# Second norm of both borders by columns: eight columns of sums, root and reciprocal, spread by a product with diagonals, and a new order list

## The chip, the cores and the metric

The kernel runs on one core of one Trainium2 chip. The metric is the time of an execution on the device in microseconds (us). TensorE is called PE here, VectorE DVE, ScalarE ACT, GpSimd POOL, and SyncE, which only issues DMAs, SP.

## The reference

One encoder layer on 512 tokens of width 1024, of three sublayers. Each has the same frame:

```
h = rms_norm(x, g) * (1 + scale) + shift
y = rms_norm(fn(h), g2)
x = x + w * gate * y
```

`fn` is a SwiGLU feed-forward in the first and third sublayer (hidden width 2816) and a mixer in the second: one projection gives queries, keys, values and two recurrent branches; four heads of differential attention and a gated recurrence in both directions run beside each other, and an output projection joins them. `scale`, `shift` and `gate` come from a conditioning vector. The norm divides each token by the root of its mean square over the 1024 channels plus 1e-6.

## The kernel before

**Layout.** Channels lie on the 128 partitions, tokens along the free dimension: the residual is a tile `X` of eight blocks (k = 0 to 7) of 128x512. A sum over channels is therefore a sum over partitions, made by PE with a matrix of ones. Each f32 product is made of three in fp32r (`mm3`, L177 to L179): high part of the weights by high part of the data, low by high, high by low. ACT makes the high part of a weight tile (L206, steps `ws`), DVE or POOL the low part (L214, steps `wl`), from a tile that a DMA staged (steps `wd`). There are three tiles of each kind, so `ws` of a unit waits until PE is done with the unit three before.

**The borders.** A border is the passage from one sublayer to the next; border 1 stands ahead of the mixer, border 2 ahead of the second feed-forward. Its steps, in the names of the code (a step is `name.border.half.block`, and `half` is left out where all 512 tokens are meant):

- `pt`: the last output tile of the sublayer, in two halves of 256 tokens. `qs` squares it on ACT; `sa` (L869) and `sn` (L872) sum the squares over the partitions on PE, `sa` those of the tiles before and `sn` that of the last one; `sq` takes the root on ACT. That is the first norm, of the sublayer's output.
- `xm`, `xf`, `xg`: `X` is scaled and the output added, on DVE or POOL. `uh` and `ul` make the high and low part of `X` for the next projection, which starts before the second norm is known: `kq` and `kk.k` multiply block k of the seven first weight tiles, and `gm.0` to `gm.6` add the last block tile by tile. The seven sums fill seven of the eight PSUM banks; `sh` (L419) makes seven columns for the shift, `sw` copies them.
- `sx`, `sax`: squares of `X` on ACT, added up on DVE or POOL. `e2` (L931, L932) makes the epsilon's share, 128x512. `ss` (L945, L946): two products with the matrix of ones put the sum of squares of each token into all 128 partitions of a bank, 128x512. `sd` (L970, DVE) scales and adds the epsilon's share, `sr` (L975, ACT) takes the root, `rv` (L978, DVE) the reciprocal, all on 128x512. That is the second norm, `r12`.
- `hm.k` (L982): `X` block k times `r12`, from SBUF; `hf`, `hh`, `hl` scale and shift it and split it into high and low part. Those are the data of the further projections (`pj`, `vp`, `tt`). The seven sums are scaled by `r12` when they are taken out of PSUM: `xs` and `rs` in border 1 (L1019), `sg` in border 2 (L1472).

**Behind border 1.** `xs.i` scales a tile of the recurrent branch, `xa.i` (ACT) adds the shift, `cd.i` is its convolution on DVE (L1274 and three L1278), `ch.i` (ACT, L1301) and `cl.i` (DVE, L811) its high and low part. `ga.ik` are the gate products of tile i, each of two times three products, with `gs` (ACT, a sigmoid) behind them. `ga.00` is the first thing that PE does after `gm.6`. The attention (`sc` scores, `mx` maxima, `ex` exponentials, `w1` and `w2` weights, `tp` transposes, `pv` values, `ms` to `mu` a norm by columns) and the recurrence (`le` to `ls`) follow, then the output projection `mo`, `mp`.

The attention's norm is already made by columns: `ms` (L1219) sums into eight columns, `me` (L1223, ACT) takes the root of 128x8, `rc` (L1227, DVE) the reciprocal, `dx` (L1233, ACT) makes four diagonals and `rb` (L1237) spreads them by one product with ones.

**The order.** Everything from the last part of the first feed-forward's output to the first tiles of the second feed-forward is issued in an order written out by hand or by a search, the list `MIXER` of some 880 steps. The program issues the steps one after another, and each engine works its own instructions off in that sequence. A suffix `.p` puts a step on POOL, `.d` on DVE. An instruction that waits holds up all that stand behind it on its engine.

Of the kernel before, what the change touches and what calls it, by code (L numbers as in the profile page):

```python
# [76 lines left out]
xm.1.1.3 gh.1 xg.1.7 xg.1.3 uh.1.2.3 xm.1.1.5 xg.1.5 wd.-1 wd.0 sax.1.1 sax.1.2 kq.1.2 kq.1.3 ws.-1 sx.1.4
sx.1.3 sx.1.5 gh.0 uh.1.2.7 ul.1.2.3 sax.1.3 wl.-1 xg.1.6 kq.1.4 sax.1.4 sax.1.5.p ul.1.2.4 kk.1.2 kk.1.3 wd.1
sx.1.6 sax.1.6 sx.1.7 sw.1 sfree.1 e2.1.p ws.0 uh.1.2.6 uh.1.2.5 wl.0 wd.2 ul.1.2.5 ws.1 ss.1 ws.2 sd.1
ul.1.2.7 sr.1 rv.1 wd.3 hm.1.1 xq kk.1.4 hf.1.1 ul.1.2.6 hm.1.3 hm.1.4 hf.1.3 hm.1.2 hh.1.1 hm.1.7 hm.1.6  # L80
gl.0.p hm.1.0 hf.1.7 wl.1.p wl.2.p ws.3 kk.1.5 wd.4 wd.5 hm.1.5 kk.1.6 hf.1.2.d wl.3 wd.6 gm.1.0 gm.1.1 gm.1.2
# [1570 lines left out]
```

## Time and profile before

| | us |
|---|---|
| median of 3 runs | 985.12 |
| lowest, highest | 984.38, 986.12 |
| the profiled execution, its own time | 985.61 |
| its span in the trace | 983.8 |
| busy in that span: PE, DVE, ACT, POOL | 957.7, 595.8, 432.3, 201.2 |

Border 1 lies at about 365 to 426 us of the span, the gates, the attention and the recurrence from there to about 573, border 2 at about 594 to 644. A row of a view gives the line of the code, the engine, the operation with what it writes and reads, the shape and how often it came; rows of the timeline give the start and the duration in us; a bracket at the end gives the idle time of the engine before the row and what ended it. Matmuls overlap, so that a row is longer than the distance to the next one; on the chain of waits each stands with the time that it adds.

### The profile page before, as it was taken

How to read it: one execution, taken by the hardware profiler on the slowest of the kernel's cores; microseconds unless marked ns; L12 is line 12 of the kernel's file. 1: busy time of each engine (PE TensorE's matmuls, PEld its weight loads, DVE VectorE, ACT ScalarE, POOL GpSimd, SP SyncE). 2: the span in 40 equal slices, each digit the busy share in tenths (PEclk: the TensorE clock that was granted, in tenths of full speed). 3: DMA queues.
4: the chain of work that ended last, by engine and by line, in shares of the span. 5: the costliest groups of instructions: out<-in, count | busy, mean ns of one | idle time of the engine just before them, and what ended most of it. 6: DMA issues, size and time to landing. Idle time of an engine off the chain costs nothing.

```text
span 983.8 us, 11742 instructions
## 1 busy us (share of the span) xinstructions
PE 957.7 (97%) x4480; PEld 789.3 (80%) x4480; DVE 595.8 (61%) x814; ACT 432.3 (44%) x668; POOL 201.2 (20%) x138
## 2 busy tenths in 40 slices
PE   7999999999999999989999999999999999999994
PEld 4888888888888889867777779788888888888883
DVE  7977656566666656998899647984333333322216
ACT  5662332335222234589988766552223322222230
POOL 1007300000000123434667332252200000001014
PEclk9999999999999999989999999999999999999998
DMA  8836555555688872223221231332232323333312
GB/s 308 313 132 231 208 185 199 201 193 176 222 277 268 291 214 67 90 64 107 78 84 32 65 121 57 102 108 90 103 107 85 108 89 99 86 95 98 97 38 86
DMA packets 45002, 137.10 MB, mean 139 GB/s; under 512 B 7185, under 2 KB 9745, under 8 KB 44946
## 3 DMA queue, kind: packets, MB, share of 16 engines
q1 hardware_dynamic: 44082, 135.62, 41.3%
q8 instruction: 35, 0.57, 0.2%
q10 hardware_dynamic: 864, 0.74, 0.2%
q14 instruction: 21, 0.17, 0.1%
HBM read 132.14 MB, written 2.10 MB: 136 GB/s over the span
## 4 chain that ended last, share of the span: by engine, by line
PE 94%; DVE 4%; DMA 1%; SPq 0%; issue 0%; ACT 0%; DVEq 0%; ACTq 0%
PE PS L177 30%; PE PS L179 30%; PE PS L178 30%; PE PS L1146 1%; PE PS L1183 1%; DVE s L1574 1%; DVE s L1577 1%; DMA X<-in_xT 1%; DVE s L1278 0%; PE PS L1219 0%; DVE s L1569 0%; PE PS L1237 0%; PE PS L476 0%; PE PS L419 0%; PE PS L872 0%; SPq L465 0%
## 5 line engine op out<-in xcount | busy, mean ns | idle before, releaser
L177 PE MATMUL PS<-s,wh 128*128 128x512 f32 (+1 forms) x1032 | 394.3, 382 | 0.1
L179 PE MATMUL PS<-s,wh 128*128 128x512 f32 (+1 forms) x1032 | 391.9, 380 | 0.0
L178 PE MATMUL PS<-s,wl 128*128 128x512 f32 (+1 forms) x1032 | 391.7, 380 | 0.0
L214 DVE TENSOR_TENSOR wl<-st,wh 128x1024 fp32r<-128x1024 f32 (+3 forms) x148 | 178.4, 1207 | 191.0 <-ACT wh L206 190.8
L206 ACT ACTIVATE wh<-st 128x1024 fp32r<-128x1024 f32 (+2 forms) x170 | 170.3, 1002 | 127.7 <-PE PS L179 115.1
L177 PEld LDWEIGHTS PS<-s,wh 128*128 128x128 f32 x1032 | 194.1, 188 | 38.7 <-issue 1.0
L179 PEld LDWEIGHTS PS<-s,wh 128*128 128x128 f32 x1032 | 194.0, 188 | 37.2 <-DVE s L542 0.4
L178 PEld LDWEIGHTS PS<-s,wl 128*128 128x128 f32 x1032 | 194.1, 188 | 36.9 <-issue 0.5
L177 PE MATMUL PS<-q,wh 128*128 128x512 f32 (+1 forms) x288 | 107.0, 371 | 0.0
L179 PE MATMUL PS<-q,wh 128*128 128x512 f32 (+1 forms) x288 | 106.0, 368 | 0.0
L178 PE MATMUL PS<-q,wl 128*128 128x512 f32 (+1 forms) x288 | 105.9, 368 | 0.0
L729 POOL TENSOR_TENSOR s<-s,s 128x512 f32<-128x512 f32 x12 | 16.1, 1341 | 385.6 <-ACT s L725 385.6
L259 DVE CUSTOM_DVE_ANT_0 q<-q,q 128x1024 bf16<-128x1024 f32 x72 | 89.7, 1246 | 0.2 <-DMA q<-in_w_ada 0.2
L649 ACT ACTIVATE s<-PS 128x512 f32<-128x512 f32 x39 | 23.3, 596 | 101.8 <-PE PS L179 101.7
L654 DVE TENSOR_TENSOR s<-s,PS 128x512 f32<-128x512 f32 x40 | 27.4, 685 | 65.9 <-PE PS L179 65.2
L214 POOL TENSOR_TENSOR wl<-st,wh 128x1024 fp32r<-128x1024 f32 (+3 forms) x21 | 50.7, 2422 | 61.0 <-ACT wh L206 61.0
L177 PEld LDWEIGHTS PS<-q,wh 128*128 128x128 f32 x288 | 54.2, 188 | 9.8 <-ACT s L1385 0.4
L179 PEld LDWEIGHTS PS<-q,wh 128*128 128x128 f32 x288 | 54.1, 188 | 9.8 <-POOL q L811 0.3
L178 PEld LDWEIGHTS PS<-q,wl 128*128 128x128 f32 x288 | 54.2, 188 | 9.6
L625 ACT ACTIVATE q<-s 128x512 fp32r<-128x512 f32 x24 | 15.2, 632 | 95.4 <-DVE s L654 95.4
L625 ACT ACTIVATE s<-s 128x512 fp32r<-128x512 f32 x16 | 10.1, 632 | 70.4 <-DVE s L654 70.4
L414 DVE SCALAR_TENSOR_TENSOR s<-st,ada,s 128x512 f32<-128x512 f32 (+1 forms) x28 | 19.7, 743 | 26.6 <-DMA st<-in_wma 13.4
(241 smaller groups left out, 922.0 us busy)
## 6 DMA issues: line engine op xcount, KB each, us to landing
q<-in_w_ada SPq DMA_DIRECT2D x72, 512.0 KB, 3.8
st<-in_w2b SPq DMA_DIRECT2D x37, 512.0 KB, 3.3
st<-in_w1b SPq DMA_DIRECT2D x36, 512.0 KB, 4.5
st<-in_w1o SPq DMA_DIRECT2D x16, 512.0 KB, 4.5
st<-in_w2o SPq DMA_DIRECT2D x16, 512.0 KB, 3.5
st<-in_wma SPq DMA_DIRECT2D x16, 448.0 KB, 4.1
st<-in_w2a SPq DMA_DIRECT2D x16, 448.0 KB, 3.4
st<-in_wmb SPq DMA_DIRECT2D x9, 512.0 KB, 3.4
```

Of the source, the lines that this page charges most:

```text
L177: PE.matmul(o, wh, ah, start=start, stop=False)
L178: PE.matmul(o, wl, ah, start=False, stop=False)
L179: PE.matmul(o, wh, al, start=False, stop=stop)
L206: ACT.activation(h[:, :n], staged[i][:, :n], AF.Copy)
L214: eng.tensor_tensor(out=l[:, :n], in0=st[:, :n], in1=h[:, :n].bitcast(F32), op=ALU.subtract)
L259: DVE.tensor_tensor_reduce(out=junk, in0=t, in1=cond, op0=ALU.mult, op1=ALU.add, scale=1.0, scalar=0.0, accum_out=ada[:, i:i + 1])
L414: DVE.scalar_tensor_tensor(out=o, in0=i, scalar=colS(j, k), in1=o, op0=ALU.mult, op1=ALU.add)
L625: ACT.activation(h, t, AF.Copy)
L649: ACT.activation(t, PS[:, b], AF.Silu)
L654: DVE.tensor_tensor(out=g, in0=g, in1=PS[:, b], op=ALU.mult)
L729: POOL.tensor_tensor(out=st["acc"], in0=st["acc"], in1=t, op=ALU.add)
L1146: PE.matmul(PS[:, b[m]], qs[x][part, c], ks[y][part], start=i == 0, stop=i == 2)
```

## The change

The second norm of both borders goes the way of the attention's norm. `e2` keeps only its first step, on one partition (1x512). `ss` becomes twelve products of two columns: for each of the four groups of 128 tokens one with the epsilon's row (one partition, against a new constant `epsd`) and two with the sums of squares, all into eight columns of one bank. `sd` is now the root of 128x8 on ACT, `sr` a reciprocal of 128x8 and four diagonals of 128x128 on DVE, `rv` one product of 128x512 on PE, which spreads the diagonals over all partitions of the same bank. `hm` reads this bank instead of a tile in SBUF and always runs on DVE; a new step `rw` copies the bank to SBUF on ACT, for `xs`, `rs` and `sg`, and a new step `ub` gives the bank back, later than before. Nothing else is computed otherwise.

```
-ws.-5 lt.1 dq pt.1.0.0 sa.1.0 wl.-5.p pt.1.0.1 pt.1.0.2 pt.1.1.0 qs.1.0 sn.1.0 pt.1.1.1 pt.1.1.2 wd.-4 wd.-3
+pt.1.0.0 ws.-5 lt.1 pt.1.0.1 wl.-5.p pt.1.0.2 wd.-4 sa.1.1 qs.1.0 sa.1.0 sn.1.0 sq.1.0 xm.1.0.0.p xm.1.0.5
...
+    epsd = one.tile([128, 2], F32, name="epsd")
...
+    DVE.memset(epsd, EPS * D)
...
         def e2(e, b):
             t, s1 = ar.s(), B["s1", b]
             G[b].E2 = t
-            e.tensor_tensor(out=t, in0=s1, in1=s1, op=ALU.mult)
-            e.tensor_scalar(out=t, in0=t, scalar1=EPS, scalar2=0.0, op0=ALU.mult, op1=ALU.add)
+            e.tensor_tensor(out=t[0:1], in0=s1[0:1], in1=s1[0:1], op=ALU.mult)
...
         def ss(e, b):
             k = G[b].sb = bank()
-            t, q = B["sx", b, 0], B["sx", b, 7]
-            PE.matmul(PS[:, k], ones, t, start=True, stop=False)
-            PE.matmul(PS[:, k], ones, q, start=False, stop=True)
-            ar.give(t, q)
+            t, q, E2 = B["sx", b, 0], B["sx", b, 7], G[b].E2
+            for a, c in ((E2[0:1], epsd[0:1]), (t, ones[:, 0:2]), (q, ones[:, 0:2])):
+                for i in range(4):
+                    PE.matmul(PS[:, k, 2 * i:2 * i + 2], a[:, 128 * i:128 * i + 128], c, start=a is not t and a is not q and i == 0,
+                              stop=a is q and i == 3)
+            ar.give(t, q, E2)
...
         def sd(e, b):
             g = G[b]
+            g.rt = smp.tile([128, 8], F32, tag="rt", name="rt", bufs=1)
+            ACT.activation(g.rt, PS[:, g.sb, 0:8], AF.Sqrt, scale=1.0 / D)
+
+        def sr(e, b):
+            g = G[b]
             g.r12 = ar.s()
-            DVE.scalar_tensor_tensor(out=g.r12, in0=PS[:, g.sb], scalar=1.0 / D, in1=g.E2, op0=ALU.mult, op1=ALU.add)
-            unbank(g.sb)
-            ar.give(g.E2)
-
-        def sr(e, b):
-            ACT.activation(G[b].r12, G[b].r12, AF.Sqrt)
+            DVE.reciprocal(g.rt, g.rt)
+            for i in range(4):
+                DVE.tensor_scalar(out=g.r12[:, 128 * i:128 * i + 128], in0=ident, scalar1=g.rt[:, 2 * i:2 * i + 1], scalar2=None,
+                                  op0=ALU.mult)
 
         def rv(e, b):
-            DVE.reciprocal(G[b].r12, G[b].r12)
+
+            PE.matmul(PS[:, G[b].sb], ones, G[b].r12, start=True, stop=True)
+
+        def rw(e, b):
+            ACT.activation(G[b].r12, PS[:, G[b].sb], AF.Copy)
+
+        def ub(e, b):
+            unbank(G[b].sb)
 
         def hm(e, b, k):
             ht[b, k] = ar.s()
-            e.tensor_tensor(out=ht[b, k], in0=X[:, k], in1=G[b].r12, op=ALU.mult)
+            DVE.tensor_tensor(out=ht[b, k], in0=X[:, k], in1=PS[:, G[b].sb], op=ALU.mult)
```

The whole list `MIXER` is another one, with 882 steps. Line numbers behind the new code are higher: by 2 or 3 in the first part, so that `mm3` is L179 to L181, `sa` L872, `sn` L875 and `sh` L422, and by 15 behind the border. In the new kernel `ss` is L950, `sd` L975, `sr` L980 and L982, `rv` L987, `rw` L990 and `hm` L997. Three places of the new order are shown. The number behind the name of a tile tells one use of a slot from another.

**PE at the second border, around `ss.2`.** First before: the last product of a block of `kk`, the two products of the sum, and the next block.

```order
L179 MATMUL PS<-s_4879,wh 128x512
L945 MATMUL PS<-s_4845,ones 128x512
L946 MATMUL PS<-s_4956,ones 128x512
L177 MATMUL PS<-s_4912,wh 128x512
L178 MATMUL PS<-s_4912,wl 128x512
L179 MATMUL PS<-s_4913,wh 128x512
```

Now the same place; `s_5046` are the four diagonals.

```order
L181 MATMUL PS<-s_4972,wh 128x512
L950 MATMUL PS<-epsd,s_5017 128x2 x4
L950 MATMUL PS<-ones,s_4963 128x2 x4
L950 MATMUL PS<-ones,s_5007 128x2 x4
L987 MATMUL PS<-s_5046,ones 128x512
L179 MATMUL PS<-s_5014,wh 128x512
L180 MATMUL PS<-s_5014,wl 128x512
L181 MATMUL PS<-s_5015,wh 128x512
```

Here `rv.2` (L987) follows `ss.2` at once, and `kk.2.4` stands behind it. `ss.2` stands behind `kk.2.3`, one block later than before. In border 1 the block `kk.1.4` stands between `ss.1` and `rv.1`.

**DVE at the first border, from the first `xs` to the low part for the gate.** Before: three scalings of tiles from PSUM, two convolutions, and the low part `cl.0` (L811).

```order
L1019 TENSOR_TENSOR s_3185<-PS,s_3057 128x512
L1019 TENSOR_TENSOR s_3188<-PS,s_3057 128x512
L1019 TENSOR_TENSOR s_3192<-PS,s_3057 128x512
L1274 TENSOR_SCALAR s_3206<-q_3066,par 128x512
L1278 SCALAR_TENSOR_TENSOR s_3206<-q_3066,par,s_3206 128x510
L1278 SCALAR_TENSOR_TENSOR s_3206<-q_3066,par,s_3206 128x511 x2
L1274 TENSOR_SCALAR s_3220<-q_3066,par 128x512
L1278 SCALAR_TENSOR_TENSOR s_3220<-q_3066,par,s_3220 128x510
L1278 SCALAR_TENSOR_TENSOR s_3220<-q_3066,par,s_3220 128x511 x2
L811 TENSOR_TENSOR s_3212<-s_3206,s_3211 128x512
```

Now (L1034 are the scalings, L216 is `wl.5`, L814 is `cl.0`):

```order
L1034 TENSOR_TENSOR s_3230<-PS,s_3095 128x512
L216 TENSOR_TENSOR wl<-st,wh 128x1024
L1034 TENSOR_TENSOR s_3242<-PS,s_3095 128x512
L1289 TENSOR_SCALAR s_3246<-q_2820,par 128x512
L1293 SCALAR_TENSOR_TENSOR s_3246<-q_2820,par,s_3246 128x510
L1293 SCALAR_TENSOR_TENSOR s_3246<-q_2820,par,s_3246 128x511 x2
L1034 TENSOR_TENSOR s_3252<-PS,s_3095 128x512
L814 TENSOR_TENSOR s_3255<-s_3246,s_3254 128x512
```

The second convolution now stands behind the low part, and the low part `wl.5` of a weight tile stands among the scalings.

**PE at the end of the sublayer's last tile, border 1, second half.** Before: the last product of the tile, `sa.1.1`, `sn.1.1`, then the columns of the shift (`sh.1`).

```order
L179 MATMUL PS<-s_1886,wh 128x256
L869 MATMUL PS<-s_1992,ones 128x256
L872 MATMUL PS<-s_2644,ones 128x256
L419 MATMUL PS<-ones,s_1963 128x2 x4
L419 MATMUL PS<-ones,s_1964 128x2 x3
```

Now:

```order
L181 MATMUL PS<-s_1888,wh 128x256
L422 MATMUL PS<-ones,s_1965 128x2 x4
L422 MATMUL PS<-ones,s_1966 128x2 x3
L875 MATMUL PS<-s_2670,ones 128x256
L179 MATMUL PS<-s_2802,wh 128x256
```

The columns of the shift moved ahead of `sn`; `sa.1.1` was made with the first half. At border 2 `sh.2` stands ahead of `sa.2.1` and `sn.2.1` too, and `pt.2.1.0` ahead of `sa.2.0` and `sn.2.0`.

More of the change, by code (lines that the diff above doesn't have):

```diff
@@ L77 @@
[L77 to L81, printed above, removed]
@@ L122 @@
[L122 to L123 removed]
+pt.1.0.0 ws.-5 lt.1 pt.1.0.1 wl.-5.p pt.1.0.2 wd.-4 sa.1.1 qs.1.0 sa.1.0 sn.1.0 sq.1.0 xm.1.0.0.p xm.1.0.5
+xm.1.0.7.p pt.1.1.0 ws.-4 pt.1.1.1 xm.1.0.1.p pt.1.1.2 lfree.1 wd.-3 wd.-2 xf.1.0.0 uh.1.0.0 xm.1.0.4
+xf.1.0.1.p uh.1.0.1 ul.1.0.0 sh.1 xm.1.0.2 xm.1.0.6 xq ul.1.0.1 ws.-3 qs.1.1 xm.1.0.3.p wl.-4 wl.-3 sn.1.1
@@ new lines @@
+ul.1.2.6 kk.1.4 gh.0 gl.0 sd.1 sr.1 ul.1.2.7 rv.1 wl.1 wd.4 wl.2 hm.1.4 kk.1.5 ws.3 hf.1.4 wl.3.p hm.1.7
+hm.1.3 hf.1.3 hm.1.0 hh.1.3 hm.1.2 hm.1.5 wd.5 hf.1.0.d kk.1.6 hh.1.4 hm.1.1 gl.1.p rawfree gm.1.0 gm.1.1
+gm.1.2 hl.1.3.p hf.1.5.d hf.1.2 gm.1.3 gm.1.4 wd.6 gm.1.5 hh.1.2 hl.1.2 hf.1.7 hl.1.4 dq gm.1.6 hh.1.7 hh.1.5
+ws.4 hm.1.6 hf.1.6 wl.4 rw.1 ws.5 xs.0 wl.5 xa.0 ub.1 hl.1.5.p hh.1.6 hh.1.0 xs.2 xa.2 hl.1.7.p cd.0 hf.1.1
+rs.k0 ch.0 cl.0 hh.1.1 hl.1.1.p xs.3 xs.1 ra.k0 rd.k0 ga.00 ws.6 rs.q1 xa.1 gs.00 rs.q0 cd.2 xa.3 ch.2 ga.01
@@ new lines @@
+wr.12 pv.2 po.2 ge.3 lh.1 ll.1 ah.0 ex.13 ll.2.p mo.0 w2.14 lf.3 w1.12 w2.12 mo.2 wr.13 mo.1 ws.20 lh.3
+wl.20.p w1.13 w2.13 wd.22 ms.2 tp.12 ex.15 tp.14 me.2 tp.13 th.13 ll.3 wr.15 ws.21 th.14 al.0 w1.15.p mo.3
+w2.15 tp.15 wd.23 ws.22 wl.21 tl.13 rc.2 ah.1 th.15 tl.14 mo.4 zF.k3 tl.15 dx.2 th.12 ws.23 wl.22.p hfree
+tl.12 wd.24 rb.2 ws.24 al.1 mu.2 ah.2 wl.23.p pv.3 lt.2 po.3 mo.5 wd.25 ws.25 wd.26 ms.3 me.3 al.2 wl.24.p
+rc.3 mo.6 dx.3 rb.3 wl.25.p mu.3 ws.26 ah.3 wd.27 al.3 mp.4 mo.7 wl.26 ws.27 mp.5 pf.0 pf.1 zF.q3 wd.28 ws.28
@@ new lines @@
+wd.29 wl.27 wl.28 vfree ws.29 mp.6 pf.2 pf.3 pt.2.0.0 pf.4 pf.5 pa.1.p pt.2.0.1 pa.2.p pt.2.0.2 wd.30 ws.30
+wd.31 pa.3.p wl.29.p pf.6 rr pa.4 pt.2.0.3 pa.5 pa.6 pt.2.1.0 sa.2.0 qs.2.0 sn.2.0 sq.2.0 wl.30 so.0 pt.2.1.1
+xm.2.0.0 qkfree.3 xf.2.0.0 uh.2.0.0 pt.2.1.2 xm.2.0.4 xm.2.0.3 pt.2.1.3 qs.2.1 xm.2.0.2 wd.32 ul.2.0.0
+xm.2.0.1 sh.2 xm.2.0.5 wd.33 sa.2.1 xf.2.0.1 sn.2.1 sq.2.1 uh.2.0.1 so.1 ws.31 xm.2.1.2 ul.2.0.1 xm.2.1.0
+xf.2.1.0.p xm.2.1.1 uh.2.1.0 xg.2.2 ul.2.1.0 xf.2.1.1.p uh.2.1.1 ul.2.1.1 xm.2.1.3 xm.2.0.6 xm.2.1.6 lfree.2
@@ L124 @@
+ws.37 hm.2.1 hm.2.6 wl.36.p hm.2.2 wd.38 hf.2.1.d hm.2.5 kk.2.6 rw.2 wd.39 gm.2.0 hf.2.2.d hh.2.2 hh.2.3
+hf.2.6 hh.2.6 gm.2.1 hl.2.3.p hl.2.4.p ws.38 wl.37 wd.40 hh.2.1 hl.2.6 gm.2.2 gm.2.3 hf.2.7 gm.2.4 hl.2.0.p
+gm.2.5 gm.2.6 sg.0 sl.0 gfree.2 hf.2.5 hh.2.5 hh.2.7 ws.39 sg.2 hl.2.1.p sg.4 hl.2.2.p sl.4 sg.5 tt.7.0 sg.3
+sg.6 sl.6 sl.2 wl.38 hl.2.5.p sg.1 ofree ub.2 pg.0 hl.2.7.p tt.7.1 ws.40 pg.1 pg.2 tt.8.0 wl.39 p3 ph.0 wd.41
+ph.3 ph.1 tt.8.1 pl.1 ph.2 wl.40 pl.2 pl.3 p4 pl.0 r2free
 """.split()
```

76 lines of the change are left out of this document (30 added, 46 removed).

## The prediction

> **What bounds the kernel now.** I read the page first, for the engine that is always busy.
>
> ```profile
> span 983.8 us, 11742 instructions
> PE 957.7 (97%) x4480; PEld 789.3 (80%) x4480; DVE 595.8 (61%) x814; ACT 432.3 (44%) x668; POOL 201.2 (20%) x138
> ```
>
> PE fills 97% of the span, so two things can move the end: products that PE gains or loses, and pauses of PE. I read the waits of PE next (line, whom it waited for, us in total, times, longest).
>
> ```profile
> PE PS L577 <- ACT s L539: 3.4, 1, 3.4
> PE PS L179 <- DVE s L811: 2.6, 1, 2.6
> ...
> PE PS L177 <- ACT s L1301: 1.8, 1, 1.8
> ```
>
> L577 lies at the start, which the change doesn't touch. Of the rest only two waits, for L1301 and L811, pass half a microsecond, and both stand at one place: the first gate product `ga.00` of the first border. Third, the chain of waits from 400 to 440 us (start, us, what):
>
> ```profile
> 404.85 0.86 PE PS L945 x2
> 405.71 0.86 PE PS L946 x2
> ...
> 421.35 0.24 PE PS L179
> 421.61 2.05 DVE s L1019 x3
> 423.66 0.47 DVE s L1274
> ...
> 426.47 0.47 DVE s L1274
> ...
> 429.29 1.69 DVE s L811
> 431.02 0.80 PE PS L179
> ...
> 435.06 0.24 PE PS L179
> ```
>
> The reader sees the norm's two products (0.86 each), PE at 0.24 per product until 421.35, and then the chain leaving PE: from the end of `gm.0` (421.59) DVE scales three tiles, makes two convolutions (`cd.0`, `cd.2`) and the low part `cl.0`, whose end at 430.98 lets PE go on. From 431.02 to 435.06 PE is at work but takes 4.04 for nine products, where nine at 0.23 are 2.07: 1.97 lost after the pause. The windows say why (PE, PEld, DVE, ACT, POOL busy; then the granted clock):
>
> ```profile
> 425.00:428.00 3.00, 1.16 (x5) 0.48 (x3) 2.90 (x5) 3.00 (x7) 0.00 (x0) 0.98 0.19 75
> 428.00:431.00 3.00, 0.40 (x1) 0.00 (x0) 2.96 (x4) 3.00 (x6) 1.33 (x1) 0.50 0.01 3
> 431.00:434.00 3.00, 2.98 (x7) 2.43 (x8) 3.00 (x5) 2.92 (x5) 2.84 (x2) 0.50 0.00 0
> ```
>
> The clock was halved from about 428 to 434 at least. The first border so holds 4.4 us of waits and 2.0 us of slow clock. The second border holds no wait of PE of this kind.
>
> **The change, part by part.** *Products.* The rows for the shapes that come (the first also for `sn`, below):
>
> ```profile
> 597.58 0.70 PE PS L872 x2
> ...
> 602.32 1.46 PE PS L419 x14
> ```
> ```profile
> 536.73 0.86 PE PS L1237 x2
> ```
>
> L419 is seven products of two columns in 1.46, 0.209 each; L1237 spreads four diagonals, just what `rv` does now. `ss` goes from 2 x 0.86 = 1.72 to 12 x 0.209 = 2.50, and `rv` adds 0.86: +1.64 a border, **+3.3** in both, all on PE and so all on the path. Four of the twelve have one partition, which no row shows; I take the same price. At nothing they would save 1.7 in both borders, and nothing in the trace suggests a price above 0.209.
>
> *DVE and ACT work.* The reciprocal of 512 columns, the scaled addition and the second step of `e2` leave DVE; a reciprocal of 8 columns and four 128x128 products come, with a copy on ACT (`rw`); `dq` merely moves. These are worth only what the chain to the gate and the chain to `rv` make of them. The rows for both:
>
> ```profile
> 409.09 3.34 DVE L978 RECIPROCAL s<-s 128x512 f32<-128x512 f32 x1
> ...
> 413.74 4.29 DVE L982 TENSOR_TENSOR s<-X,s 128x512 f32<-128x512 f32 x7
> 417.95 0.54 DVE L989 TENSOR_SCALAR s<-s,aA,ada 128x512 f32<-128x512 f32 x1
> ```
> ```profile
> 402.34 0.16 DVE L425 COPY bc<-PS 128x14 f32<-128x14 f32 x1
> ```
> ```profile
> 568.73 0.20 DVE L1227 RECIPROCAL rm<-rm 128x8 f32<-128x8 f32 x1 [5.99 <-ACT rm L1223]
> ```
> ```profile
> 568.43 0.27 ACT L1223 ACTIVATE rm<-PS,epsc 128x8 f32<-128x8 f32 x1
> ```
>
> *First border.* `rv` stands behind `kk.1.4`, 21 products or 4.8 us after `ss`. Root (0.27), reciprocal (0.20) and diagonals need 1.5 (below), behind `gl.0` on DVE, so `rv` is covered; without that cover it would cost the 1.5. But `hm` still begins about 6 us after the sums: the 3.34 went, and PE's 4.8 took its place. What DVE gains is the time before it, into which the order puts `wl.1` and `wl.2`. After it come eight `hm` (0.61 each by the L982 row), scalings, low parts and `wl.4`, some 8 us, and then a wait for `gm.0`, whose end is 1.64 later than before; about 1 us is left there. So the pause at the gate hangs, as before, on what DVE does between `gm.0` and `cl.0`. Before: 430.98 - 421.59 = 9.4. Now: `xs.0`, `wl.5`, `xs.2`, `cd.0`, `rs.k0`, `cl.0`, with `cd.2` behind them.
>
> ```profile
> 637.77 1.23 DVE L214 TENSOR_TENSOR wl<-st,wh 128x1024 fp32r<-128x1024 f32 x1 [0.21 <-ACT wh L206]
> ```
> ```profile
> 435.20 0.68 DVE L811 TENSOR_TENSOR s<-s,s 128x512 fp32r<-128x512 f32 x1
> ```
>
> Three L1019 take 2.05, so 0.66 each; `wl.5` 1.15 net of overlap; `cd.0` 426.47 - 423.66 = 2.81; `cl.0` 0.68, since the 1.69 before stood beside a POOL operation (1.33 busy in the window from 428) and POOL now reaches its next low part only after `hh.1`. With 0.1 of hand-overs: 3 x 0.66 + 1.15 + 2.81 + 0.68 + 0.1 = 6.7. `ch.0`, on ACT, hides beside `rs.k0`. The chain shrinks by 9.4 - 6.7 = **-2.7**; some 2.2 us of pause stay, about 1.9 at the first product and 0.3 at the third.
>
> *Second border.* Here `rv` follows `ss` on PE with nothing between. Behind it on PE wait `kk.2.4` and everything else. The wait: root 0.27, reciprocal 0.20, four diagonals. The L425 and L989 rows bound one diagonal by 0.16 and 0.54; a quarter of L989's columns puts it at 0.25, four at 0.76 with overlap. With hand-overs of 0.04 each and the start of the product: **+1.5**, bounds 1.2 and 2.9. No later wait gives that back: before, this border had none.
>
> *Start of the borders.* `sn` took 0.70 where its twin `sa` takes 0.43 (382.50), at three places (382.97, and both halves of the second border, as at 597.58), since the square had only just been asked for. Now the shift products or the next part stand ahead of each.
>
> ```profile
> 382.50 0.43 PE PS L869 x2
> 382.93 0.04 issue
> 382.97 0.70 PE PS L872 x2
> ```
>
> Worth 3 x 0.27 at most; I take **-0.6**, bounds 0 and -0.8.
>
> *Clock.* The lost 1.97 goes only if the clock now stays up. In the rows, PE was busy 1.16 of the three us before the drop, so no wholly idle stretch was needed. A pause of 2.2 at the gate, and in the second border 2.5 of two-column products and 1.5 of waiting, can each bring a drop. I take one drop in all, at the old price: **0**, bounds -2.0 (none) and +2.0 (two). By the Trainium skill, TensorE: Matmul & The Clock Gate, Part 1, the half clock comes after an idle window of about 3.4 us, free-running. By that rule neither pause is long enough, and the sum would be 2.0 lower; the trace doesn't agree, as it dropped after 1.84 and then 2.62 idle with products between.
>
> *The sum.* 3.3 - 2.7 + 1.5 - 0.6 + 0 = **+1.5 us**. The profiled execution took 985.61 (span 983.8 and 1.8 around it), 0.5 above the median of 985.12; against the median the forecast is **986.6 us**.
>
> **The rivals.** *The clock holds* at both places: 1.5 - 2.0 = -0.5, 984.6, no change. For it: each pause is shorter than the 4.4 of before. Chance 0.25. The rule of the Trainium skill above comes out this way.
>
> *Slower by two drops.* The two-column products leave PE nearly as idle as a wait, so that the 2.5 + 1.5 at the second border halves the clock there and the gate's pause does it too: 1.5 + 2.0 = +3.5, 988.6. It decides where PE's busy share of some 3 us falls under what dropped it before, 1.16 of 3. Against, the window with the 1.46 of L419, at full clock:
>
> ```profile
> 600.00:605.00 5.00, 4.96 (x39) 4.50 (x38) 4.97 (x16) 1.91 (x5) 0.62 (x1) 1.00 0.06 22
> ```
>
> Chance 0.25.
>
> *Slower in the attention.* Before, all four `le` on ACT stood ahead of `sc.1`; now two stand behind it, while PE comes 1 to 3 us earlier.
>
> ```profile
> 450.00:460.00 10.00, 10.00 (x50) 7.76 (x49) 7.87 (x11) 9.76 (x17) 5.86 (x5) 1.00 0.36 123
> ```
>
> ACT is full (9.76 of 10), so PE could get its lead back as a wait for `ex`, up to 3: 989.6. Against: both orders leave the same sum of ACT work. Chance 0.05.
>
> *Faster.* The gate's pause goes wholly, if DVE's chain hides behind `gm`: 3.3 - 4.4 - 2.0 + 1.5 - 0.6 = -2.2, 982.9. Against it the 6.7, where `gm.1` to `gm.6` and two products cover 18 x 0.23 + 0.46 = 4.6. Chance 0.05.
>
> **How the numbers follow.** The forecast has 0.40. 0.2% is 1.97 us, about what a measurement of this kernel can tell. The forecast's +1.5 with its bounds lies within it in 0.28 of its 0.40 and above in 0.12. The clock's rival adds 0.24 to same and 0.01 to faster; the two slower rivals add 0.30; the faster one 0.05. So faster 0.06, same 0.52, slower 0.42. The range reaches from just under the clock's rival, 984.0, to the upper rivals with a little on top, 989.5; outside lie the faster rival and the worst of the others.
>
> **What would show it.** Right: L950 rows of about 0.2 each; one wait of PE at the second L987 for DVE of about 1.5; waits at the first gate product of about 1.9 and 0.3; `sn` rows of 0.43. The granted clock per window tells the rivals apart. Wrong: a pause at the gate under 1 or over 3.5, a wait at the first L987, new waits of PE over 1 us between 450 and 560, or an L950 price off by half.

## The result, and the profile after

The kernel became slower: 990.39 us in the median of five runs (989.19 to 992.57), against 985.12 (984.38 to 986.12) of the kernel before. The ratio is 1.0053, its 95% interval 1.0040 to 1.0067. The forecast was 986.6 with a range up to 989.5. The profiled execution of after is the slowest of its five, 992.57; it lies 7.0 us above that of before (985.61), so the profile shows more loss than the median of the runs, 5.3.

The page of after, its first lines:

```profile
span 990.7 us, 11837 instructions
PE 965.8 (97%) x4524; PEld 796.4 (80%) x4524; DVE 593.5 (60%) x810; ACT 432.3 (44%) x669; POOL 209.9 (21%) x148
```

PE is still busy for 97% of the span, and its busy time grew by 8.1 us while the span grew by 6.9. So the loss is not to be looked for in idle time alone. The waits of PE (line, whom it waited for, us in total, times, longest):

```profile
PE PS L580 <- ACT s L542: 3.4, 1, 3.4
...
PE PS L179 <- ACT s L1316: 2.0, 1, 2.0
PE PS L987 <- DVE s L982: 1.5, 1, 1.5
```

The two waits that the prediction named are there, with its sizes: 2.0 at the first gate product (before 1.8 there and 2.6 at the third), 1.5 at the second border's spread product. There is none at the first L987, and none in the attention. The chain of waits at the first border (start, us, what) shows the rest:

```profile
404.96 2.86 PE PS L950 x24
407.81 0.34 PE PS L179
...
408.99 0.43 PE PS L180
...
414.33 0.86 PE PS L987 x2
...
431.48 0.50 PE PS L179
...
432.80 0.43 PE PS L179
...
436.34 0.23 PE PS L179
```

From 408.99 on the products of `kk.1.4` take 0.43 instead of 0.23, although PE has waited for nothing here; behind the gate's pause they do so once more. At the second border:

```profile
627.13 0.19 ACT rt L975
...
627.34 0.21 DVE rt L980
...
627.58 0.89 DVE s L982 x4
...
628.60 2.04 PE PS L987 x2
630.64 0.43 PE PS L179
...
634.02 0.23 PE PS L181
```

Root, reciprocal and diagonals are the wait as it was added up, but the spread product behind them takes 2.04, where the one at the first border takes 0.86, and eight more products some 0.43 each. The windows over these places (PE, PEld, DVE, ACT, POOL busy, then the granted clock):

```profile
405.00:408.00 3.00, 3.00 (x26) 2.94 (x27) 2.27 (x3) 2.04 (x3) 0.00 (x0) 1.00 0.00 0
408.00:411.00 3.00, 3.00 (x10) 2.32 (x9) 2.96 (x9) 0.03 (x1) 0.00 (x0) 0.59 0.03 8
428.00:432.00 4.00, 2.01 (x9) 1.21 (x7) 3.80 (x6) 2.61 (x6) 0.00 (x0) 1.00 0.00 0
432.00:436.00 4.00, 4.00 (x11) 2.97 (x11) 3.93 (x8) 3.98 (x5) 2.53 (x2) 0.57 0.26 64
627.00:630.00 3.00, 1.49 (x4) 0.84 (x4) 1.74 (x6) 2.46 (x4) 1.17 (x1) 0.50 0.01 5
630.00:634.00 4.00, 4.00 (x10) 2.79 (x9) 3.32 (x6) 2.00 (x3) 1.05 (x1) 0.52 0.36 131
```

The clock was halved in three stretches, where the kernel before had one. The first comes behind a window in which PE is busy 3.00 of 3.00: what it was busy with were the twelve products of two columns.

Where the time went can be counted on PE alone. Both kernels issue the same 4,200 fp32r products (L177 to L179 and L577 of before). At full clock they follow each other at 0.227 us; half of that, 0.113, is taken for those of 256 columns. The table shows, by stage in us, the time between the first and the last start of PE that goes beyond this: all other products of PE, the waits and the slow stretches.

| stage of the span | before | after | e7 | e14 | e11 |
|---|---|---|---|---|---|
| to 365 | 18.9 | 19.1 | 18.5 | 18.5 | 17.4 |
| border 1 and gates, to 445 | 13.7 | 14.3 | 12.3 | 12.4 | 11.5 |
| attention, to 595 | 31.1 | 31.4 | 31.8 | 31.4 | 32.4 |
| border 2, to 655 | 6.5 | 12.1 | 11.1 | 11.1 | 7.7 |
| to the end of PE | 4.2 | 4.1 | 4.1 | 4.1 | 4.1 |

Of 6.6 us, 5.6 were lost at the second border; the other 0.3 of the span is that PE starts its first product later. At the first border the shorter pause nearly paid for the sums and their slow stretch. (The last three columns are experiments, below.)

### The profile page after: what moved, and what is told of

It reads as the page before. It is cut to its first block, busy times and chain, and to the rows that moved or that the text cites. A ratio compares the mean times of both kernels' runs of the same rounds, so it can differ in the third digit from the quotient of the medians.

```text
span 990.7 us, 11837 instructions
## 1 busy us (share of the span) xinstructions
PE 965.8 (97%) x4524; PEld 796.4 (80%) x4524; DVE 593.5 (60%) x810; ACT 432.3 (44%) x669; POOL 209.9 (21%) x148
## 4 chain that ended last, share of the span: by engine, by line
PE 90%; DVE 5%; ACT 3%; issue 1%; DMA 1%; SPq 0%; DVEq 0%; ACTq 0%
PE PS L179 29%; PE PS L180 29%; PE PS L181 29%; PE PS L1161 1%; PE PS L1198 1%; DVE s L1589 1%; DVE s L1293 1%; DVE s L1592 1%; PE PS L950 1%; DVE wl L216 1%; ACT s L1174 1%; DMA X<-in_xT 1%; PE PS L479 1%; ACT wh L208 0%; PE PS L1252 0%
## 5 line engine op out<-in xcount | busy, mean ns | idle before, releaser
L179 PE MATMUL PS<-s,wh 128*128 128x512 f32 (+1 forms) x1032 | 395.7, 383 | 0.1
L181 PE MATMUL PS<-s,wh 128*128 128x512 f32 (+1 forms) x1032 | 392.9, 381 | 0.0
L216 DVE TENSOR_TENSOR wl<-st,wh 128x1024 fp32r<-128x1024 f32 (+3 forms) x150 | 182.1, 1216 | 192.6 <-ACT wh L208 192.6
L179 PEld LDWEIGHTS PS<-s,wh 128*128 128x128 f32 x1032 | 194.9, 189 | 38.9 <-issue 1.5
L181 PEld LDWEIGHTS PS<-s,wh 128*128 128x128 f32 x1032 | 194.9, 189 | 37.3 <-DVE s L545 0.4
L179 PE MATMUL PS<-q,wh 128*128 128x512 f32 (+1 forms) x288 | 106.8, 371 | 0.0
L181 PE MATMUL PS<-q,wh 128*128 128x512 f32 (+1 forms) x288 | 105.8, 367 | 0.0
L261 DVE CUSTOM_DVE_ANT_0 q<-q,q 128x1024 bf16<-128x1024 f32 x72 | 92.0, 1278 | 0.1
L179 PEld LDWEIGHTS PS<-q,wh 128*128 128x128 f32 x288 | 54.3, 188 | 9.9 <-issue 0.2
L181 PEld LDWEIGHTS PS<-q,wh 128*128 128x128 f32 x288 | 54.1, 188 | 9.5
L216 POOL TENSOR_TENSOR wl<-st,wh 128x1024 fp32r<-128x1024 f32 (+3 forms) x19 | 39.8, 2096 | 62.0 <-ACT wh L208 59.7
L417 DVE SCALAR_TENSOR_TENSOR s<-st,ada,s 128x512 f32<-128x512 f32 (+1 forms) x28 | 17.9, 682 | 29.5 <-DMA st<-in_w2a 16.1
```

What stands on the lines that cost most here:

```text
L179: PE.matmul(o, wh, ah, start=start, stop=False)
L181: PE.matmul(o, wh, al, start=False, stop=stop)
L216: eng.tensor_tensor(out=l[:, :n], in0=st[:, :n], in1=h[:, :n].bitcast(F32), op=ALU.subtract)
L261: DVE.tensor_tensor_reduce(out=junk, in0=t, in1=cond, op0=ALU.mult, op1=ALU.add, scale=1.0, scalar=0.0, accum_out=ada[:, i:i + 1])
L417: DVE.scalar_tensor_tensor(out=o, in0=i, scalar=colS(j, k), in1=o, op0=ALU.mult, op1=ALU.add)
```

## The experiments

The theory that the profile suggests: for the clock, products of two columns count as standing still, so that twelve of them in a row halve it as a pause does, and the forecast's one slow stretch became three. The rivals: only a pause of PE halves the clock, and the slow products behind the first sums have another cause; or the new order loses by itself. Each run below stands beside runs of the kernel before on the same chip (medians of 985.3 to 986.0), and ratios are to those.

**e1: runs of two columns by themselves.** Products whose results nobody uses, put into the kernel before where PE never waits (one run; a second helper, for the run with wide products between, is left out here).

```
+        def dz(e, n, w, p):
+            for i in range(n):
+                j = i // 8 % 4 * 128
+                PE.matmul(PS[:, pfree[0], 0:w], X[0:p, i % 8, j:j + 128], ones[0:p, 0:w], start=True, stop=True)
...
```

> The kernel before, with runs of idle products (results not used) put between products of the attention where TensorE never waits: 4, 8, 12, 12, 16, 24, 8 and 12 products of two columns, 12 of 128 columns, 12 of two columns from one partition, and 12 of two columns each followed by a product of 512 columns. Theory (products of two columns count as standing still for the clock): the granted clock halves for about 3.4 us behind the runs of 12, 16 and 24 (2.9, 3.8 and 5.8 us long at the 0.24 us of after), not behind 4 (1.0 us), behind 8 (1.9 us) by where they fall; not behind the run with 512-column products between. Rival (only a wait of TensorE drops the clock): 1.00 behind all of them, and the slow products behind the first sums of after come from something else at that place. The time says little: some 30 us more of products by both, and 1.7 us more for each drop.

The clock halved behind the runs of 16 and of 24, behind the run from one partition (the attention's own four sums follow it at once, so that 3.9 us of two-column products lie together there), and behind two of three runs of twelve. It held behind 4, behind both of 8, behind twelve of 128 columns and behind twelve with a 512-column product after each. In the windows, a run of twelve that dropped it (469.19 to 472.04) and the one that did not (484.41 to 487.01):

```profile
469.00:472.00 3.00, 3.00 (x26) 2.96 (x25) 3.00 (x7) 2.90 (x6) 0.00 (x0) 0.92 0.50 173
472.00:475.00 3.00, 3.00 (x8) 2.42 (x9) 3.00 (x6) 2.98 (x7) 0.00 (x0) 0.51 0.02 7
484.00:487.00 3.00, 3.00 (x27) 2.92 (x26) 1.20 (x3) 2.33 (x4) 3.00 (x4) 1.00 0.10 22
487.00:490.00 3.00, 3.00 (x15) 2.49 (x15) 3.00 (x2) 2.49 (x3) 3.00 (x2) 1.00 0.29 66
```

What parts them is when they came. The windows in which the five drops begin:

```profile
471.00:472.00 1.00, 1.00 (x9) 1.00 (x9) 1.00 (x4) 0.97 (x3) 0.00 (x0) 0.76 0.87 344
498.00:499.00 1.00, 1.00 (x10) 1.00 (x10) 0.00 (x0) 0.99 (x2) 0.00 (x0) 0.91 0.29 66
519.00:520.00 1.00, 1.00 (x8) 1.00 (x8) 0.21 (x1) 0.00 (x0) 1.00 (x1) 0.65 0.36 84
546.00:547.00 1.00, 1.00 (x9) 1.00 (x9) 0.84 (x1) 0.00 (x0) 1.00 (x2) 0.80 0.00 0
604.00:605.00 1.00, 1.00 (x5) 0.78 (x4) 0.00 (x0) 0.00 (x0) 0.00 (x0) 0.82 0.87 336
```

A mean of 0.76 between 1.00 and 0.50 puts the edge at 471.52; the others come at 498.82, 519.30, 546.60 and 604.64. They lie 27.3, 47.8, 75.1 and 133.1 us behind the first, which is 8, 14, 22 and 39 times 3.413. So the clock is decided at the edges of a grid of 3.41 us. A stretch from one edge to the next is called a cell below, and the question is how much of one cell passes without wide products. The run at 469.19 had 2.3 us in the cell that ended at 471.52; that at 484.41 had 0.8 and 1.8 on the two sides of the edge at 485.17; one at 600.66 had 2.0 (601.23 to 603.26) and dropped it. Runs of two columns do count as standing still; the rival that only waits do is out.

The traces of all 17 kernels of this case, from 100 to 960 us, say the same. Take for each cell at full clock the time in which no product of 128 columns or more runs (each of these taken with its time back to back), so that pauses and two-column products stand together. In 32 cells this time was 2.1 us or more, and behind every one the clock halved; in the other 4,079 it was 2.0 or less, and it halved behind none. The drop of before fits too, with 2.1 us of pause in the cell that ended at 427.9.

**e2: the spread product of border 2 behind other products.** After, with `kk.2.4` cut into its seven tiles (`kp`), three of them ahead of `rv.2`, and what these need put early.

```
-sax.2.6 ss.2 ... sr.2 ul.2.2.4 ws.34 ws.35 rv.2 hm.2.4 hm.2.0 wl.33.p ... kk.2.4
+sax.2.6 ul.2.2.4 ss.2 ... sr.2 ws.34 ws.35 wl.33.p kp.2.4.0 kp.2.4.1 kp.2.4.2 rv.2 hm.2.4 hm.2.0 ... kp.2.4.3 ... kp.2.4.6
```

> After, with the second border's spread product behind the first nine products of the next k (2.1 us) and that k's low part made ahead of the diagonals. Both theories: the wait of 1.5 us at L987 goes. Theory (the twelve sums alone drop the clock there): one slow stretch of 3.4 us stays instead of one of 6.9, so 1.5 + about 0.8 less: 988.1 us (987.4 to 988.9). Rival (the wait drops the clock): no slow stretch is left at the second border, 1.5 + 2.5 less: 986.4 us.

990.15 us, ratio 1.0048 (1.0036 to 1.0060). The wait at L987 went, and one slow stretch of 3.4 us (626.0 to 629.4) stayed behind the twelve sums alone. But a new wait stood at 634.73:

```profile
PE PS L181 <- DVE s L441: 1.2, 1, 1.2
```

It is for the low part `ul.2.2.5`, now behind the normalised tiles on DVE. Mechanism as expected, gain given back; e14 takes this wait away.

**e14: the same without the new wait.**

```
-sr.2 ... wl.34.p ul.2.2.6 ... ul.2.2.7 ... hh.2.0 ul.2.2.5
+sr.2 ul.2.2.5 ul.2.2.6 ul.2.2.7 ... wl.34.p ... hh.2.0
```

> The second experiment (after with the spread product of the second border behind nine products of the next k) with the low parts of the three k behind it ahead of its use on VectorE, where the new wait of 1.2 us stood. Theory: no wait at the second border; the slow stretch there is that of the twelve sums alone, one window where it comes at all: TensorE's time beside the main products there from 12.1 us to 9.8, 988.0 us. Rival (the second border's wait moves on once more): 989.5 us or more with a wait of 1 us or more between 625 and 650 us.

987.93 us, 1.0024 (1.0014 to 1.0034). No wait is left at the second border, yet the clock drops there:

```profile
620.00:623.00 3.00, 3.00 (x20) 2.44 (x18) 3.00 (x2) 0.85 (x2) 1.81 (x1) 1.00 0.09 18
623.00:627.00 4.00, 4.00 (x18) 3.61 (x18) 1.80 (x8) 2.02 (x4) 0.31 (x1) 0.59 0.27 101
627.00:630.00 3.00, 3.00 (x8) 1.99 (x6) 3.00 (x2) 0.45 (x1) 1.94 (x1) 0.50 0.06 11
```

PE is busy all through, and the slow stretch is two cells long here, so the stage fell only from 12.1 to 11.1 instead of 9.8. By the medians (1.0053 of after, 1.0024 here) about half of the loss went with the wait; this trace, from one of the slower of twelve runs that spread over 5.2 us, shows less. What stays is the sums and the slow stretch behind them.

**e3: four sums at each border.** The last squares added on DVE, the epsilon row added into one partition of them.

```
+            DVE.scalar_tensor_tensor(out=q[0:1], in0=t[0:1], scalar=EPS * D, in1=q[0:1], op0=ALU.mult, op1=ALU.add)
...
-            for a, c in ((E2[0:1], epsd[0:1]), (t, ones[:, 0:2]), (q, ones[:, 0:2])):
...
+            for i in range(4):
+                PE.matmul(PS[:, k, 2 * i:2 * i + 2], t[:, 128 * i:128 * i + 128], ones[:, 0:2], start=i == 0, stop=i == 3)
...
-... e2.1 sax.1.2
+... e2.1 sax.1.7 sax.1.2
```

> After, with 4 sum products at each border instead of 12: the last squares are added on VectorE, and the epsilon row is added into one partition of the squares. Both: 8 products of 0.24 us less at each border, 3.8 us. Theory (the run of sums drops the clock): the slow stretch behind the first border's sums goes (1.7 us), that of the second border becomes shorter or goes (1.0 us of sums and 1.5 us of waiting are left): 984.9 us, down to 983 if it goes. Rival (waits alone): the slow stretches stay, 986.6 us.

989.81 us, 1.0040 (1.0027 to 1.0053). The slow stretch behind the first border's sums went. But DVE now ends late:

```profile
PE PS L952 <- DVE s L928: 3.8, 2, 2.9
```

The two additions on DVE stand in the chain ahead of the sums, and 2.9 us of the waiting is at the second border. There eight products less save nothing, as DVE pays for them: the clock drops for two cells behind the wait (623.2 to 630.0).

**e6: the same with the row on GpSimd.** The edit is against e3.

```
-            DVE.scalar_tensor_tensor(out=q[0:1], in0=t[0:1], scalar=EPS * D, in1=q[0:1], op0=ALU.mult, op1=ALU.add)
+            e.tensor_scalar(out=t[0:1], in0=t[0:1], scalar1=EPS * D, scalar2=0.0, op0=ALU.mult, op1=ALU.add)
+            e.tensor_tensor(out=q[0:1], in0=q[0:1], in1=t[0:1], op=ALU.add)
-e2.1 ... e2.2
+e2.1.p ... e2.2.p
```

> The four sums of the third experiment, with the epsilon row worked out and added on GpSimd, so that VectorE has one operation of 0.67 us less than there and as many as after. Both: the waits of 0.9 and 2.9 us for the sums go or shrink below 1 us together. Theory (a run of short products of 1 us cannot drop the clock): no slow stretch behind the first border's sums in any run; at the second border 1.0 us of sums and 1.5 us of waiting may or may not drop it: 984.5 us, 986.5 with the drop. Rival (VectorE stays late by the one sum more): the wait at the sums stays at 2 us or more, 988 us.

996.07 us, 1.0103 (1.0089 to 1.0117). The rival, and worse than it: the waits at the sums grew to 6.2 us. DVE's chain of additions stood behind POOL (a wait of 4.2 us for its row at the first border), and beside POOL's operations DVE itself slows down, as the last section shows.

**e4 and e7: the gate earlier.** Shown is e7 against after. In e4 `gm.1.0` comes right behind the first tile of `kk.1.6`, and DVE's chain `xs.0`, `cd.0`, `cl.0` ahead of `wl.4` and `wl.5`; in e7 the copy `hh.1.1` goes ahead of `ch.0` on ACT, and `xs.2` behind `cl.0` on DVE, as well.

```
-kk.1.6 ... gm.1.0 gm.1.1
+kp.1.6.0 gm.1.0 kp.1.6.1 ... kp.1.6.6 ... gm.1.1
-ws.4 hm.1.6 hf.1.6 wl.4 rw.1 ws.5 xs.0 wl.5 xa.0 ... xs.2 xa.2 hl.1.7.p cd.0 hf.1.1 rs.k0 ch.0 cl.0 hh.1.1 hl.1.1.p
+rw.1 ws.4 xs.0 hm.1.6 xa.0 cd.0 hf.1.6 wl.4 ... hf.1.1 hh.1.1 hl.1.1.p ch.0 cl.0 hl.1.7.p xs.2 ws.5 xa.2 wl.5 rs.k0
```

> After, with the first tile's last products 4 us earlier among those of the k before, and VectorE's chain to the first gate (normalise, convolve, low part) ahead of two weight splits. Theory (the pause at the gates hangs on that chain, and the clock on the pause): the wait of 2.0 us goes with the slow stretch of 1.8 us behind it, 986.6 us. Rival (something else holds the gate, or the chain's place is taken by a later wait for the delayed splits): the wait stays or returns at the next projection, 989 to 991 us.

e4: 989.66 us, 1.0049 (1.0037 to 1.0061). The pause of 2.0 became 0.5, and 2.8 us came at the next projection. The clock stayed up behind it:

```profile
430.93 0.40 PE L180 MATMUL PS<-s,wl 128*128 128x512 f32 x1
434.09 0.50 PE L181 MATMUL PS<-s,wh 128*128 128x512 f32 x1 [2.76 <-POOL s L814]
```
```profile
431.00:435.00 4.00, 1.24 (x6) 0.78 (x5) 3.93 (x5) 3.98 (x6) 2.69 (x2) 1.00 0.20 49
```

By the drop at 627.0 in the same trace an edge lay at 432.4, in the middle of this pause: 1.3 us on one side (431.2 to 432.4, from where the last product would have been followed by the next), 1.7 on the other. After's pause of 2.0 lay in one cell and dropped it.

> The early gate of the fourth experiment, with the copy of the second tile's high part on ScalarE, on which GpSimd's low part waited there, ahead of the copy for the gate. Theory (the 2.8 us at the next projection were that copy, queued behind ScalarE's wait): the wait goes, TensorE waits less than 1 us in all between 420 and 445 us, no slow stretch there; 986 us, 1.7 more where the run of twelve sums drops the clock at the first border. Rival (the delayed weight splits or GpSimd are late anyway): a wait of 1.5 us or more stays at that projection, 988.5 us.

e7: 989.15 us, 1.0034 (1.0022 to 1.0045). The 2.8 went, four waits of 0.3 to 1.0 came; stage 12.3. The gain is some 0.2% against after, but the second border still has its 11.1.

**e5 and e10: the old norm in the new order.** e5 is the kernel before with after's list (without `rw` and `ub`); e10 is e7 with the old norm at the second border alone.

```
-MIXER of before
+MIXER of after, less rw.1 rw.2 ub.1 ub.2
```

> The kernel before, its norm unchanged (two sum products of 512 columns, the reciprocal of 128x512 on VectorE), in the order of after (the two steps that before does not have are left out of it). Theory (the new norm on TensorE costs what was lost: 12 short products and a spread product at each border, the wait of 1.5 us and the slow stretches behind the runs of sums; the new order by itself gains at the gates): after's 990.4 less 2.3 for the sums, 1.7 for the spread products, 1.5 for the wait, 1.7 and 2.5 for the two slow stretches: 980.7 us, up to 983 if the reciprocal of 3.34 us pushes the gate chain back. Rival (the new order loses by itself, the norm is neutral): 988 us or more.

e5: 996.70 us, 1.0107 (1.0092 to 1.0123). The expectation of 981 failed. PE waits 4.0 us for a weight split, 3.7 at the gate and 3.7 for low parts: in this order the reciprocal of 3.34 us stands ahead of two weight splits on DVE, which the chain of waits passes through. So the new order does not suit the old norm; what the order alone costs with the new norm, this run doesn't show.

> The seventh experiment (new norm at both borders, early gate) with the norm of before at the second border alone: two sum products of 512 columns, sum, root and reciprocal on VectorE and ScalarE over 128x512, the epsilon row on GpSimd, and the low parts of the next three k on VectorE ahead of the reciprocal. Theory (what was lost lies at the second border, in the twelve sums, the wait for the spread product and the slow stretch they cause): TensorE's time there beside the main products goes from 11.1 us to about 6.5 as in before, 984.5 us. Rival (the second border loses by the order that after brought there): it stays at 9 us or more, 988 us.

e10: 990.23 us, 1.0047 (1.0033 to 1.0060); border 2 at 11.6 where 6.5 was expected. The sums are short and no stretch is slow, but waits of 1.5 us for a weight split and 2.2 for low parts took their place. This run doesn't part the norm from the order.

**e9: the kernel before with the early gate.** Its own norm, `gm.1.0` early (for that its weights are copied behind `kk.1.4` and split on POOL), `cl.0` ahead of `cd.2`.

```
-... xs.0 xa.0 xs.1 ... cd.0 ch.0 hh.1.0 hh.1.3 cd.2 hh.1.2 wl.4.p hh.1.7 ch.2 cl.0
+... xs.0 xa.0 ... cd.0 ... ch.0 xs.1 xs.2 cl.0 ... cd.2 ... ch.2
```

> The kernel before with its own norm, the first tile's last products early among those of the k before, its weights copied earlier and split on GpSimd, and VectorE's chain to the first gate (normalise, convolve, low part) ahead of the second tile's. Theory (the pause at the gates depends on the order of that chain and not on the norm): the waits of 1.8 and 2.6 us go, and the slow stretch of 2.0 us with them; up to 2 us come back as a wait at the second gate tile: 981 us (979.5 to 983.5). Rival (with the long norm the chain cannot be early enough): the waits stay above 3 us together, 984 us or more.

984.60 us, 0.9994 (0.9985 to 1.0003): no difference that can be measured. The pause fell from 4.4 to 2.4 us, smaller waits of 1.1 came behind, and the clock still dropped, for one cell instead of two. This is the rival.

**e8, e11 and e12: the cures together.** e8 joins e7, e6's four sums and e14's place for `rv.2`. e11 has eight sums, with POOL adding the row to an early square that is not last in DVE's chain. e12 is e11 with three steps of the order moved. First e11's edit of `e2`, then e12's of the order.

```
+            q = B["sx", b, 7 if b == 1 else 1]
+            POOL.tensor_tensor(out=t[0:1], in0=s1[0:1], in1=s1[0:1], op=ALU.mult)
+            POOL.tensor_scalar(out=t[0:1], in0=t[0:1], scalar1=EPS * D, scalar2=0.0, op0=ALU.mult, op1=ALU.add)
+            POOL.tensor_tensor(out=q[0:1], in0=q[0:1], in1=t[0:1], op=ALU.add)
```
```
-xs.2 ws.5 xa.2 wl.5 rs.k0 xs.3 xs.1
+xs.2 ws.5 xa.2 rs.k0 xs.3 xs.1 wl.5
...
-sax.1.2 wl.0
+sax.1.2 wl.0.p
...
-e2.2 xm.2.1.7 ... wl.31
+e2.2 ... wl.31 xm.2.1.7
```

> After with the four sums (GpSimd's epsilon row), the spread product behind nine products with the next low parts ahead of it on VectorE, and the early gate. Theory: against after 3.8 us for the sums, 1.5 and 2.0 for the waits, 1.7, 1.8 and 2.5 for the slow stretches, 977 us, up to 981 with one wait or one slow stretch left; faster than the kernel before by 0.4 to 0.8 per cent. Rival (each cure moves the wait to another place): 985 us or more, and the profile shows waits of 3 us or more between 395 and 640 us.

e8: 993.79 us, 1.0077 (1.0064 to 1.0090). It has all of e6's waits at the sums, 6.2 us together. This is the rival.

> The seventh experiment with the new norm kept at both borders, but eight sums instead of twelve (the epsilon row added on GpSimd into one partition of an early square, nothing more on VectorE), and at the second border the spread product behind nine products of the next k with the low parts of four k ahead of its use. Theory: a run of eight (1.9 us) stays under what drops the clock and the wait is filled: at the second border 1.9 + 0.5 us for sums and spread product, no wait over 0.5 us and no slow stretch, 11.1 us become 7.7; at the first border 0.9 us less: 984.8 us. Rival (the wait moves to the low parts or the normalised tiles, as in the second experiment): a wait of 1.2 us or more stays at the second border, 986.5 us or more.

e11: 985.69 us, 0.9998 (0.9990 to 1.0007): all of the loss is back. At the second border the clock holds:

```profile
620.00:624.00 4.00, 3.96 (x26) 3.35 (x25) 3.86 (x6) 2.78 (x6) 2.35 (x1) 1.00 0.04 6
624.00:628.00 4.00, 4.00 (x18) 2.90 (x17) 4.00 (x6) 1.43 (x2) 2.47 (x1) 1.00 0.32 108
```

Against e7 the stage went from 11.1 to 7.7, the number that the theory had given, but with some luck: a product of `sa` (0.4 us) falls just ahead of 595 in this trace, so that 8.1 is the like figure, and a wait of 0.9 us for a weight split stays, longer than the theory allowed. With the early gate it makes the new norm as fast as the kernel before, not faster.

> The eleventh experiment with three places of its order changed: at the gates VectorE splits the second weight only after the normalised tiles that free banks (a wait of 0.92 us there), at the first border GpSimd instead of VectorE splits one weight that stood ahead of the sums (a wait of 0.42 us at the sums), at the second border one short product on VectorE goes behind a weight split (a wait of 0.87 us). Theory (what is left over the kernel before are these waits and 1.1 us of short products): 1.5 us less than the eleventh, 984.2 us, faster than the kernel before by 0.1 to 0.2 per cent. Rival (the waits move on to the next place, as in the second, third and fourth experiments): 985.5 us or more.

e12: 989.58 us, 1.0037 (1.0023 to 1.0050), with 5.2 us between its fastest and slowest run. DVE came late to both sums, so that a wait and a run of eight lay side by side:

```profile
PE PS L953 <- DVE s L928: 2.9, 2, 1.6
```

1.3 and 1.6 us of waiting and 1.9 of short products pass 2.0 us in one cell, and the clock dropped at both borders: 16.1 and 10.9 us by stage, 4.6 and some 2.8 more than in e11. So in this trace, of the slowest run of the five, the stages lost clearly more than the waits are long.

**e13: the run alone, added to before.**

```
+            for i in range(12):
+                PE.matmul(PS[:, k, 0:2], q[:, i % 4 * 128:i % 4 * 128 + 128], ones[:, 0:2], start=True, stop=True)
```

> The kernel before with twelve idle products of two columns (results overwritten) ahead of its own sums at each border, nothing else changed. Both: 2.8 us of TensorE at each border, 5.6 us. Theory (such a run drops the clock when 2.0 us or more of it fall into one window of 3.4 us; worked out from the first experiment, 6 times in 10): 1.7 us more for each drop, so 5.6 + about 2.1, 993.3 us with a spread of 3 us between runs, and a slow stretch behind the run at one border or at both. Rival (the clock falls only where TensorE waits): 991.2 us, no slow stretch behind the runs.

991.69 us, 1.0057 (1.0045 to 1.0069), so 5.7 us for 24 products that take 5.2 by their starts. No stretch is slow behind either run:

```profile
407.00:410.00 3.00, 3.00 (x13) 1.86 (x13) 0.66 (x2) 0.00 (x0) 3.00 (x2) 1.00 0.18 44
...
625.00:628.00 3.00, 3.00 (x11) 1.78 (x11) 1.22 (x2) 0.49 (x1) 0.00 (x0) 1.00 0.08 32
```

By this trace's drop at 432.6 the edges lay at 405.3 and 623.7: 2.0 us at most fell into one cell at the first border, 1.5 at the second. That fits the grid, but the time, over five runs that lie within 1.2 us, is the rival's number: drops were rarer than the 6 in 10 of the expectation. How often a run of twelve drops the clock, and why these runs escaped, is left open.

**e15: all twelve sums, but apart.** On e7's gate and e14's second border. Twelve sums as in after; eight of them at the first border and four at the second stand singly between the products of `kk.1.3` and `kk.2.3`.

```
+kp.1.3.0 se.1.0.0 kp.1.3.1 se.1.0.1 se.1.1.0 kp.1.3.2 ...
+kp.2.3.3 se.2.0.0 kp.2.3.4 se.2.0.1 kp.2.3.5 se.2.0.2 kp.2.3.6 se.2.0.3
```

> The seventh experiment's early gate and the fourteenth's second border, with all twelve sums kept, but the row's and the last squares' eight at the first border, and the row's four at the second, put one by one between the 512-column products of the k before: four and eight stay together at the end. TensorE issues the same products as in after. Theory (only a run together drops the clock): no slow stretch at either border; against the eleventh experiment 1.9 us more for 8 sums, 0.4 to 0.9 less for a wait at the first border's sums and a wait for a weight at the second, where GpSimd's row held VectorE: 986.6 us (985.5 to 988). Rival (the sums cost the clock wherever they stand): slow stretches at both borders, 989.5 us or more.

989.18 us, 1.0034 (1.0022 to 1.0046), 2.6 more than expected. At the first border the clock held; at the second it dropped at 628.2, since the last single product ran on into the eight: nine together, 2.1 us in the cell from 624.8.

```profile
405.00:409.00 4.00, 4.00 (x26) 3.60 (x27) 1.45 (x3) 0.75 (x1) 0.00 (x0) 1.00 0.00 0
...
628.00:631.00 3.00, 3.00 (x9) 2.38 (x8) 2.96 (x7) 2.09 (x3) 1.67 (x1) 0.53 0.00 0
```

The first border bears the theory out; the second shows how near the bound it had been cut.

## Why the prediction was wrong

**Products: right in kind, too small.** On the chain of waits the sums went from 1.72 (two rows of 0.86 in the prediction) to 2.86, and the spread product of the first border adds 0.86, as forecast (both rows above). So a product of two columns took 0.24 and not 0.209, and a border pays 2.0 instead of 1.64: 4.0 in both, not 3.3. Those from one partition are no cheaper, as the starts in the timeline of after show, 0.98 for four and 1.81 for eight:

```profile
404.89 1.05 PE L950 MATMUL PS<-epsd,s 1*128 1x2 f32 x8
405.87 1.95 PE L950 MATMUL PS<-ones,s 128*128 128x2 f32 x16
407.68 0.48 PE L179 MATMUL PS<-s,wh 128*128 128x512 f32 x1
```

**The gate: right.** -2.7 was forecast; 4.4 us of waits became 2.0, which is -2.4, all at the first product. The forecast's 0.3 at the third did not come.

**The spread product: right.** +1.5 forecast, 1.5 measured.

**`sn`: right.** Its products now take 0.43, as its twin's (in after `sa` is L872 and `sn` L875):

```profile
599.20 0.43 PE PS L872 x2
599.63 0.43 PE PS L875 x2
```

By starts, `sa` and `sn` together take 2.9 instead of 3.8, -0.9 where -0.6 was taken.

**The clock: wrong, and this is the step that failed.** The forecast took "one drop in all, at the old price", 0. After has three. From the chain: 21 products between 407.81 and 414.33 take 6.5 instead of 4.8; twelve from 431.48 to 436.34 take 4.9 instead of 2.7, some 0.3 of it the filling of PE after the pause; the second border's spread product and eight more end at 634.02, 5.4 us after the first began, where 0.86 and eight times 0.23 make 2.7. That is 1.7, 1.9 and 2.7, together 6.3 against 2.0 before: +4.3. With 4.0 - 2.4 + 1.5 - 0.9 for the other terms it makes +6.5, of the 6.6 that the table counts. This is the profiled execution, the slowest of five; in the median one the loss is 1.7 smaller, and no trace shows which of the terms is smaller there.

The prediction held two of the three causes in its hands. It priced the sums by L419, and put into a rival that two-column products may leave PE as idle as a wait; against it stood one window at full clock around the 1.46 us of L419. That row could not decide: e1 shows up to 1.8 us of a run in one cell without a drop, and 2.0 to 2.3 with one. The rival was counted as two drops, with none for the first border's sums, and given 0.25. Its measure, though, was nearly the right one: PE busy 1.16 of 3.00 is 0.39, and with 2.0 to 2.1 us of a cell without wide products some 0.4 of it is left. What the forecast lacked was to count the sums as a pause at both borders; the rival did so at the second alone.

By the Trainium skill, TensorE: Matmul & The Clock Gate, Part 1, the clock follows a free-running window of 3413 ns; the edges of e1 agree, at 8, 14, 22 and 39 times 3.413 us. The same section has the half clock come after an idle window, and there the trace doesn't agree: some 2.0 to 2.1 us of a cell were enough, and products of two columns counted as idle. The second of the two pauses that the prediction named, 2.62, came after the drop of before and was not needed for it: by its windows the clock was at 0.98 up to 428.

**The rivals.** *The clock holds* failed with the step above. *Slower in the attention* did not come: no wait of PE stands there, and the stage is at 31.4 against 31.1. *The gate's pause goes wholly* did not come in after.

What e11 shows: with eight sums, the wait filled and the gate early, nothing of the loss remains, and the second border stands at 8.1 instead of 12.1, by the like count. What stays open is how the loss divides from run to run. It hangs on where the edges of the grid fall, and that is luck: after's five runs spread over 3.4 us, before's over 1.7.

## What to carry to other kernels

When PE's work is cut into very narrow products, price the run twice: by its own length, and as if PE stood still, together with any wait beside it. If some 2 us of narrow products and waits can meet in one cell of 3.4 us, add the slow products behind them, or put wide ones between and into the wait. A wait that is filled, or sums that are saved, are worth nothing while the engine that pays for it (DVE here) is the next one that PE waits for.
